# Second block: masked columns left out, and each head's values and their rests side by side in one stationary operand

## The chip, the cores and the metric

The kernel runs on one core of a Trainium2 chip. The metric is the device time of one execution in microseconds (us). The engines are TensorE (PE in the rows, its weight loads PEld), VectorE (DVE), ScalarE (ACT), GpSimd (POOL) and SyncE (SP, which issues the DMA transfers).

## The reference

Two blocks follow each other, each of two layers; 256 tokens of width 1024. The change touches the second block alone. A layer of it is a feed-forward part, a mix of three attention branches, and a second feed-forward part, each with a layer norm. The mix:

```python
o_a = _nsa(q_a, kv_a, g_a, ...)          # 8 heads in 2 groups: compressed, selected and window attention, gated
o_b = _swa_sink(q_b, k_b, v_b, sinks, rel_b)   # 8 heads in 2 groups: the last 128 keys, with a sink
o_c = _fox(q_c, k_c, v_c, f_c, b_f)            # 8 heads: causal, with a forget gate added to the logits
g = jax.nn.sigmoid(h @ w_gate + b_gate).reshape(B, S, N_BRANCH, D)
merged = g[:, :, 0] * (o_a @ w_br_a) + g[:, :, 1] * (o_b @ w_br_b) + g[:, :, 2] * (o_c @ w_br_c)
return merged @ w_out
```

All three branches are causal: a query of the first 128 tokens sees no key of the second 128. With 256 tokens the selection of branch a takes every block, so each branch is a softmax over at most 256 keys (and 30 compressed ones in a), with heads of 64 columns.

## The kernel before

Everything that TensorE multiplies in the stages of the change is held as a pair of fp32r numbers: a value rounded to fp32r (`h`, hi) and its rest (`l`, lo). `split` makes such a pair from a source with a cast on ScalarE (line 536) and a subtraction on VectorE (line 537). A product is three matmuls, hi by hi, hi by lo and lo by hi (`mm3`, lines 547 to 549). Weights come from memory in chunks of 128x1024; class `Weights` loads them and splits them too, on ScalarE (line 354) and VectorE (line 356), into five buffers in these stages.

`mix` makes the attention stages of a layer. Each of the three branches has 8 units, one for each head, in pairs j of two heads i; the two heads of a pair stand in the two halves of the 128 partitions. A unit goes through these steps, in `simple` for b and c and written out at the end of `mix` for a:

- `soft`: the scores of 2 x 128 queries against 256 keys (b: lines 1685 and 1686, in c also 1689; a: lines 1847 and 1851), then masked minimum (line 625), exponential (615, in a 1863), sum and reciprocal (616), and scaling (621, in a 1872) on VectorE and ScalarE. For the first 128 queries only the first 128 keys matter; the score matmuls make all 256 columns, and softmax reads 128 of them.
- the turn: three transposes of 128x128 (1710, in a 1883) bring the three weight tiles that are not masked into a bank; `split` brings them to `p_h` and `p_l`, into columns 128 to 511 of a buffer of `pts` whose first 128 columns were cleared once (line 1652) and stand for the masked tile.
- the values: for each of the two key tiles an `mm3` of 256 query columns, with the value columns of both heads of the pair as stationary operand (128 columns). So each unit computes the products of both heads, and half of the rows of its result are not used.
- `pair_out`, after the second head of a pair: the used half of the rows of each head is split into the branch's output pair.

Between these steps `fill` inserts matmuls of other work that doesn't depend on the unit: the projections of the next branch, the compression network, and the gated output projection of the branch before (`branch_job`). A scheduler then sets the order on each engine. The bank of the results (`po`) is a single one; the scores have two banks, the transposes two.

Of the kernel before, what the change touches and what calls it, by code (L numbers as in the profile page):

```python
# [475 lines left out]
HEAD = slice(0, 64), slice(64, 128)  # L476


class Kern:
# [979 lines left out]
    def mix(self, l, xh, xl, mid):  # L1459
        nc, fa, ra, d = self.nc, self.fa, self.ra, self.d  # L1460
        V, A, G, PE = nc.vector, nc.scalar, nc.gpsimd, nc.tensor
# [24 lines left out]
        vswb, vsh, vsl = parts(256)  # L1486
        qbb, qb = rows(512)
        kkb, kk = rows(384)
        vbb, vbh, vbl = parts(P)

        def evac0(t, ps):
            A.copy(kcv[:, t], ps[:, :256])
            self.split(ps[:, 256:], vsh[:, t], vsl[:, t])

        def evac2(t, ps):
            A.copy(kk[:, t, 0:P], ps[:, 0:P])
            self.split(ps[:, P:2 * P], vbh[:, t], vbl[:, t])
            A.copy(kk[:, t, P:], ps[:, 2 * P:])
# [9 lines left out]
        ct, pickb = ra.alloc(S), ra.alloc(8)  # L1508
        pick = pickb.a
# [3 lines left out]
        def gf_job():  # L1513
# [27 lines left out]
            for t in range(2):  # L1541
# [8 lines left out]
        vcb, vch, vcl = parts(512)  # L1550
# [3 lines left out]
                              lambda t, ps: self.split(ps, vch[:, t], vcl[:, t]))]  # L1554
# [5 lines left out]
        vcmp = ra.alloc(P)  # L1560
        self.clear(vcmp.a)
        kcmpb = ra.alloc(64)
# [23 lines left out]
        def cmp_job(z):  # L1586
            b = ftb[z]
            bank = self.banks[2]
            for c in range(4):
                hi, lo = self.W.take(f"cw{l}", 4 * z + c)  # L1590
                for jj in range(4):
                    j = 4 * c + jj
# [11 lines left out]
            ps = self.scr.next()[0:30, :S]  # L1604
# [8 lines left out]
            bank = self.pt.next()  # L1613
# [10 lines left out]
            if z == 0:  # L1624
                self.split(bank[:, 0:30], kcmpb.a[:, 0:30], kcmpb.a[:, 32:62])
            else:
                A.copy(vcmp.a[0:30], bank[0:30, 0:P])
                A.copy(vcmp.a[32:62], bank[0:30, 0:P])
                V.tensor_tensor(vcmp.a[64:94], bank[0:30, 0:P], vcmp.a[0:30].bitcast(F32), ALU.subtract)
# [43 lines left out]
        def simple(prep, vh, vl, paired, og, extra):  # L1673
# [5 lines left out]
            def soft(u):  # L1679
# [3 lines left out]
                for qt in range(2):  # L1683
                    qq, o = q[:, qt * P:qt * P + P], bank[:, qt * P:qt * P + S]
                    PE.matmul(o, qq, kh, start=True, stop=False)
                    PE.matmul(o, qq, kl, start=False, stop=extra is None)
                    if extra:
                        n = P if qt == 0 else S
                        PE.matmul(bank[:, qt * P:qt * P + n], pick[:, h:h + 1].to_broadcast([P, P]), extra[:, 0:n],
                                  start=False, stop=True)  # L1690
# [12 lines left out]
            for n, u in enumerate(units):  # L1703
# [8 lines left out]
                self.split(bank[:, 0:384], p_h.a[:, P:], p_l.a[:, P:])  # L1712
# [7 lines left out]
                c = slice(j * P, j * P + P) if paired else slice(0, P)  # L1720
                o = self.obank[:, i * S:i * S + S]
# [23 lines left out]
        simple(prep_b, vbh, vbl, False, og, None)  # L1745
# [62 lines left out]
        simple(prep_c, vch, vcl, True, og_c, ct.a)  # L1808
# [8 lines left out]
        W1 = 288  # L1817
# [23 lines left out]
        def soft(u):  # L1841
# [3 lines left out]
            for qt in range(2):  # L1845
                for z in range(2):
                    PE.matmul(bs[:, 160 * qt:160 * qt + W1], q[:, qt * P:qt * P + P], sl4[:, i, z],
                              start=z == 0, stop=z == 1)
            for qt in range(2):
                for z in range(2):  # L1850
                    PE.matmul(bw[:, P * qt:P * qt + S], q[:, qt * P:qt * P + P], wi4[:, i, z],
                              start=z == 0, stop=z == 1)
# [23 lines left out]
        for n, u in enumerate(units):  # L1876
# [3 lines left out]
            for k, (s, o, w) in enumerate(((s1, 160, 32), (s2, P, 0))):  # L1880
# [4 lines left out]
                self.split(bank[:, 0:384], pts[k][0].a[:, P:], pts[k][1].a[:, P:])  # L1885
# [77 lines left out]
```

## Time and profile before

| | before |
|---|---|
| time, median of 3 runs | 2344.83 us (2343.74 to 2349.3) |
| profiled execution, its time | 2346.41 us |
| its span, first to last instruction | 2344.6 us |
| TensorE busy | 2261.1 us, 96% |
| VectorE busy | 1696.6 us, 72% |
| ScalarE busy | 1249.1 us, 53% |
| DMA | 362.98 MB, 155 GB/s on average |
| granted TensorE clock | 0.993 |

Busy time counts a matmul from its start to its modelled end, and successive matmuls overlap, so what a matmul costs in a stream is read from the starts, not from its duration. The attention stages of the second block lie at about 1212 to 1430 us (layer 0) and 1890 to 2100 us (layer 1).

### The profile page before, as it was taken

What the parts mean: (1) busy time and instruction counts of PE and PEld (TensorE: products, weight loads), DVE (VectorE), ACT (ScalarE), POOL (GpSimd) and SP (SyncE); (2) the same over time, 40 slices, a digit from 0 to 9 for tenths busy, and PEclk for the clock granted to TensorE, in tenths of its full rate; (3) what the DMA queues carried; (4) which work ended last, traced back from release to release, by engine and by line L of the source; (5) the groups of instructions that cost most, each with busy time, mean ns of one, the idle gap of its engine ahead of it and who ended that gap; (6) DMA issues with size and microseconds to landing.
All of it is one profiled execution on the core that took longest, in us unless ns stands there. A gap on an engine that the chain in (4) does not pass through costs nothing.

```text
span 2344.6 us, 32027 instructions
## 1 busy us (share of the span) xinstructions
PE 2261.1 (96%) x11612; PEld 1858.8 (79%) x11612; DVE 1696.6 (72%) x3192; ACT 1249.1 (53%) x2235; POOL 244.0 (10%) x265
## 2 busy tenths in 40 slices
PE   6999899999999999999999999999999999999998
PEld 3888787787778899888877777788788877777887
DVE  6598999677689997655577897755655677897554
ACT  6385673242347864444367785444444376764452
POOL 1302200222220202200000000000000000000000
PEclk9999999999999999999999999999999999999999
DMA  8121224355443335555646435556556545445554
GB/s 321 45 82 41 75 81 135 126 165 168 134 139 110 103 132 171 179 186 180 220 137 205 138 117 173 179 188 197 189 190 219 163 153 184 144 131 179 189 190 134
DMA packets 102975, 362.98 MB, mean 155 GB/s; under 512 B 11936, under 2 KB 13088, under 8 KB 102304
## 3 DMA queue, kind: packets, MB, share of 16 engines
q1 hardware_dynamic: 102816, 360.93, 46.5%
q8 instruction: 91, 1.49, 0.3%
q14 instruction: 68, 0.56, 0.1%
HBM read 359.84 MB, written 1.05 MB: 154 GB/s over the span
## 4 chain that ended last, share of the span: by engine, by line
PE 55%; DVE 8%; ACT 4%; DMA 3%; issue 2%; POOL 1%; DVEq 0%; ACTq 0%; POOLq 0%; SPq 0%
PE bank L547 17%; PE bank L549 17%; PE bank L548 16%; DVE ra_t L356 2%; ACT ra_t L354 1%; DMA fa_t<-in_gate 1%; PE bank L1402 1%; DVE ra_t L537 1%; DVE fa_t L625 1%; DVE fa_t L1339 1%; DMA fa_t<-in_n 1%; PE bank L1265 1%; ACT ra_t L536 1%; POOL fa_t L543 0%; ACT fa_t L1863 0%
## 5 line engine op out<-in xcount | busy, mean ns | idle before, releaser
L547 PE MATMUL bank<-ra_t 128*128 128x512 f32 (+1 forms) x3216 | 1186.9, 371 | 14.3 <-DVE fa_t L786 5.0
L549 PE MATMUL bank<-ra_t 128*128 128x512 f32 (+1 forms) x3216 | 1172.8, 366 | 8.3 <-DVE ra_t L537 3.8
L548 PE MATMUL bank<-ra_t 128*128 128x512 f32 (+1 forms) x3216 | 1174.6, 367 | 3.8 <-DVE ra_t L537 1.3
L356 DVE TENSOR_TENSOR ra_t<-fa_t,ra_t 128x1024 fp32r<-128x1024 f32 x583 | 722.2, 1241 | 349.1 <-ACT ra_t L354 333.6
L354 ACT CAST ra_t<-fa_t 128x1024 fp32r<-128x1024 f32 x606 | 633.2, 1048 | 602.2 <-PE bank L549 284.5
L547 PEld LDWEIGHTS bank<-ra_t 128*128 128x128 f32 x3216 | 605.4, 189 | 129.1 <-ACT ra_t L536 15.4
L549 PEld LDWEIGHTS bank<-ra_t 128*128 128x128 f32 x3216 | 605.6, 189 | 108.7 <-DVE ra_t L537 7.3
L548 PEld LDWEIGHTS bank<-ra_t 128*128 128x128 f32 x3216 | 607.2, 189 | 103.1 <-DVE ra_t L356 5.1
L865 DVE SCALAR_TENSOR_TENSOR fa_t<-fa_t 128x512 f32<-128x512 f32 (+1 forms) x240 | 161.5, 673 | 6.0 <-ACT fa_t L863 2.8
L537 DVE TENSOR_TENSOR ra_t<-bank,ra_t 128x512 fp32r<-128x512 f32 (+5 forms) x234 | 131.2, 568 | 44.0 <-ACT ra_t L536 41.1
L536 ACT CAST ra_t<-bank 128x512 fp32r<-128x512 f32 (+5 forms) x234 | 112.8, 488 | 84.8 <-PE bank L549 33.4
L543 POOL TENSOR_TENSOR fa_t<-fa_t 128x1 f32<-128x1 f32 (+2 forms) x54 | 69.0, 1278 | 762.3 <-DVE fa_t L542 762.1
L625 DVE CUSTOM_DVE_ANT_0 fa_t<-bank,fa_t 128x256 f32<-128x256 f32 (+2 forms) x320 | 117.0, 396 | 8.7 <-PE bank L1231 1.9
L615 ACT ACTIVATE fa_t<-fa_t 128x257 f32<-128x257 f32 (+5 forms) x160 | 91.5, 574 | 21.4 <-DVE fa_t L625 20.1
L1410 ACT ACTIVATE fa_t<-bank 128x256 f32<-128x256 f32 x88 | 33.9, 385 | 112.5 <-PE bank L549 112.4
L356 POOL TENSOR_TENSOR ra_t<-fa_t,ra_t 128x1024 fp32r<-128x1024 f32 x23 | 58.0, 2520 | 276.1 <-ACT ra_t L354 273.0
L1412 DVE TENSOR_TENSOR fa_t<-fa_t,bank 128x256 f32<-128x256 f32 x88 | 36.8, 418 | 65.7 <-ACT fa_t L1410 65.5
L1184 DVE SCALAR_TENSOR_TENSOR fa_t<-fa_t 128x512 f32<-128x512 f32 x98 | 71.0, 757 | 2.3 <-DMA fa_t<-in_ada 2.0
L1053 POOL TENSOR_TENSOR fa_t<-fa_t 128x512 f32<-128x512 f32 (+1 forms) x32 | 37.3, 1172 | 154.4 <-DVE fa_t L1052 154.4
L638 DVE TENSOR_TENSOR ra_t<-bank,ra_t 64x256 fp32r<-64x256 f32 (+1 forms) x96 | 43.5, 455 | 8.3 <-ACT ra_t L637 5.3
L649 POOL CAST ra_t<-fa_t 64x256 fp32r<-64x256 f32 (+3 forms) x40 | 24.0, 606 | 241.4 <-PE bank L1597 69.9
L1863 ACT ACTIVATE fa_t<-fa_t 128x32 f32<-128x32 f32 (+2 forms) x96 | 39.0, 409 | 14.5 <-DVE fa_t L625 13.9
(218 smaller groups left out, 1701.9 us busy)
## 6 DMA issues: line engine op xcount, KB each, us to landing
fa_t<-in_f1w SPq DMA_DIRECT2D x132, 512.0 KB, 4.2
fa_t<-in_f2w SPq DMA_DIRECT2D x132, 512.0 KB, 4.3
fa_t<-in_tr SPq DMA_DIRECT2D x88, 512.0 KB, 3.5
fa_t<-in_n SPq DMA_DIRECT2D x56, 512.0 KB, 3.6
fa_t<-in_ada SPq DMA_DIRECT2D x48, 512.0 KB, 4.5
fa_t<-in_gate SPq DMA_DIRECT2D x48, 512.0 KB, 3.7
fa_t<-in_nat SPq DMA_DIRECT2D x36, 512.0 KB, 4.2
fa_t<-in_proj SPq DMA_DIRECT2D x24, 512.0 KB, 3.5
```

Of the source, the lines that this page charges most:

```text
L354: nc.scalar.copy(hi, raw)
L356: eng.tensor_tensor(lo, raw, hi.bitcast(F32), ALU.subtract)
L536: self.nc.scalar.copy(hi, src)
L537: self.nc.vector.tensor_tensor(lo, src, hi.bitcast(F32), ALU.subtract)
L543: self.nc.gpsimd.tensor_tensor(out, out, self.nhalf[:, :n], ALU.pow)
L547: mm(ps, lh, rh, start=start, stop=False)
L548: mm(ps, lh, rl, start=False, stop=False)
L549: mm(ps, ll, rh, start=False, stop=stop)
L615: nc.scalar.activation(s[:, :width or n], s[:, :width or n], AF.Exp, bias=mneg, scale=-1.0, accum_out=r)
L625: self.nc.vector.tensor_tensor_reduce(out=out, in0=a, in1=b, op0=ALU.add, op1=ALU.min, scale=-1.0, scalar=init, accum_out=acc)
L865: V.scalar_tensor_tensor(y4, src, w, y4, ALU.mult, ALU.add)
L1184: V.scalar_tensor_tensor(acc[s].a, wk, self.sc[:, kt, s:s + 1], acc[s].a, ALU.mult, ALU.add)
```

## The change

Three things change in `mix`, in both layers. First, the values of a head (64 columns) and their rests (64 columns) are stored side by side, as one stationary operand of 128 columns; `pairs` and `values` lay them out so that head 0 of a pair has its values in the first half and head 1 in the second. A key tile then takes two matmuls, with `p_h` and with `p_l` as moving operand, and the result has the part from the values in the head's own half of the partitions and the part from the rests in the other half; `pair_out` adds the two. (The product of rest and rest, which was left out before, is now in it.) Secondly, masked tiles are left out: scores of the first 128 queries are made for 128 keys only, and the second key tile is multiplied for the second 128 queries only, so that the cleared columns of `pts` go. Thirdly, the values of the compressed keys (`vcmp`) are laid out in the same way.

```diff
-        def parts(n):
-            b = ra.alloc(4 * n)
-            v = b.v("p (z t c) -> p z t c", z=2, t=2)
-            return b, v[:, 0], v[:, 1]
+        def pairs(n):
+            b = ra.alloc(512 * n)
+            return b, b.v("p (t j z c) -> p t j z c", t=2, j=n, z=4)
+
+        def values(src, v):
+            self.split(src.rearrange("p (j i c) -> p j i c", i=2, c=64), v[:, :, 0:4:3], v[:, :, 1:3])
...
-        pts = []
-        for i in range(2):
-            b = (ra.alloc(512), ra.alloc(512))
-            for z in b:
-                V.tensor_copy(z.a[:, 0:P], self.zero[:, 0:P])
-            pts.append(b)
+        pts = [(ra.alloc(3 * P), ra.alloc(3 * P)) for _ in range(2)]
...
+        def weigh(o, v, i, ps, start, stop):
+            st = v[:, 2 * i:2 * i + 2].rearrange("p z c -> p (z c)")
+            for k in range(2):
+                PE.matmul(o, st, ps[k], start=start and k == 0, stop=stop and k == 1)
...
-            for k, r in enumerate((slice(0, 64), slice(64, 128))):
-                self.split(bank[r, k * S:k * S + S], h[r, c], lo[r, c])
+            z = self.scr.next()[:, :S]
+            for k, (own, other) in enumerate((HEAD, HEAD[::-1])):
+                A.copy(z[own], bank[other, k * S:k * S + S])
+            for k, own in enumerate(HEAD):
+                V.tensor_tensor(z[own], bank[own, k * S:k * S + S], z[own], ALU.add)
+            self.split(z, h[:, c], lo[:, c])
...
-                    PE.matmul(o, qq, kh, start=True, stop=False)
-                    PE.matmul(o, qq, kl, start=False, stop=extra is None)
+                    n = P if qt == 0 else S
+                    PE.matmul(o, qq, kh[:, :n], start=True, stop=False)
+                    PE.matmul(o, qq, kl[:, :n], start=False, stop=extra is None)
...
-                for kt in range(2):
-                    r = slice(S - kt * S, 2 * S - kt * S)
-                    self.mm3(o, vh[:, kt, c], vl[:, kt, c], p_h.a[:, r], p_l.a[:, r], kt == 0, kt == 1)
+                for kt, r in enumerate((slice(P, 3 * P), slice(0, P))):
+                    weigh(self.obank[:, i * S + kt * P:i * S + S], v[:, kt, j if paired else 0], i,
+                          (p_h.a[:, r], p_l.a[:, r]), kt == 0, kt == 1)
...
-                    PE.matmul(bs[:, 160 * qt:160 * qt + W1], q[:, qt * P:qt * P + P], sl4[:, i, z],
+                    PE.matmul(bs[:, 160 * qt:160 * qt + 32 + n], q[:, qt * P:qt * P + P], sl4[:, i, z, :32 + n],
...
-                    PE.matmul(bw[:, P * qt:P * qt + S], q[:, qt * P:qt * P + P], wi4[:, i, z],
+                    PE.matmul(bw[:, P * qt:P * qt + n], q[:, qt * P:qt * P + P], wi4[:, i, z, :n],
...
-                for kt in range(2):
-                    r = slice(S - kt * S, 2 * S - kt * S)
-                    c = slice(k * P, k * P + P)
-                    self.mm3(o, vsh[:, kt, c], vsl[:, kt, c], pts[k][0].a[:, r], pts[k][1].a[:, r],
-                             k == 0 and kt == 0, False)
-            PE.matmul(o, vcmp.a, pc, start=False, stop=True)
+                for kt, r in enumerate((slice(P, 3 * P), slice(0, P))):
+                    weigh(o[:, kt * P:], vsw[:, kt, k], i, [z.a[:, r] for z in pts[k]], k == 0 and kt == 0, False)
+            PE.matmul(o, vcmp.a[:, i * P:i * P + P], pc, start=False, stop=True)
```

How this stands in the order of instructions is shown at two places. The first is TensorE in branch c of layer 0, around the seventh unit. In the kernel before, its six score matmuls (lines 1685, 1686 and 1689 into bank_66) are followed by these rows; bank_64 takes filler, bank_70 the values of the unit before.

```order
L1689 MATMUL bank_66<-ra_t 128x256
L547 MATMUL bank_70<-ra_t 128x256
L549 MATMUL bank_64<-ra_t 128x512
L547 MATMUL bank_64<-ra_t 128x512
L548 MATMUL bank_64<-ra_t 128x512
L549 MATMUL bank_64<-ra_t 128x512
L548 MATMUL bank_70<-ra_t 128x256
L549 MATMUL bank_70<-ra_t 128x256
L547 MATMUL bank_70<-ra_t 128x256
L548 MATMUL bank_70<-ra_t 128x256
L549 MATMUL bank_70<-ra_t 128x256
L547 MATMUL bank_64<-ra_t 128x512
```

Behind them stand the six score matmuls of the eighth unit (into bank_67) and then these rows, which end with the seventh unit's transposes.

```order
L1689 MATMUL bank_67<-ra_t 128x256
L548 MATMUL bank_64<-ra_t 128x512
L549 MATMUL bank_64<-ra_t 128x512
L547 MATMUL bank_64<-ra_t 128x512
L548 MATMUL bank_64<-ra_t 128x512
L549 MATMUL bank_64<-ra_t 128x512
L1710 MATMUL bank_68<-fa_t 128x128 x3
```

In the changed kernel these are the rows from the seventh unit's last score matmul (line 1703, before 1689) to its transposes (line 1723, before 1710), but for the first eight of them, which are four value matmuls (line 1675, of 256, 256, 128 and 128 columns) and the first four of the eighth unit's scores.

```order
L1701 MATMUL bank_67<-ra_t 128x256
L1703 MATMUL bank_67<-ra_t 128x256
L549 MATMUL bank_63<-ra_t 128x512
L547 MATMUL bank_64<-ra_t 128x512
L1723 MATMUL bank_68<-fa_t 128x128 x3
```

Six value matmuls have become four, and of ten filler matmuls of 512 columns between the scores and the transposes two are left; the others now stand elsewhere.

The second place is VectorE at `pair_out`, in the same branch. bank_70 holds the result of a pair. In the kernel before, each head's subtraction (line 537) reads the bank by itself:

```order
L537 TENSOR_TENSOR ra_t<-bank_70,ra_t 64x256
```

There are two such rows for a pair. In the changed kernel there are two additions (line 1684) and a subtraction over all partitions:

```order
L1684 TENSOR_TENSOR fa_t<-bank_70,fa_t 64x256 x2
...
L537 TENSOR_TENSOR ra_t<-fa_t,ra_t 128x256
```

The reads of the bank stay two, of the same shape, and a third instruction is added that doesn't read it.

## Rows read from the trace of the kernel before

**Rows 1.** The page: span, and busy us of each engine with its share and instructions.

```profile
span 2344.6 us, 32027 instructions
PE 2261.1 (96%) x11612; PEld 1858.8 (79%) x11612; DVE 1696.6 (72%) x3192; ACT 1249.1 (53%) x2235; POOL 244.0 (10%) x265
```

**Rows 2.** Windows: start:end, length, busy us of each engine, clock, DMA share, GB/s.

```profile
1221.00:1257.00 36.00, 34.77 (x204) 27.49 (x203) 31.18 (x101) 30.88 (x74) 3.37 (x13) 1.00 0.40 129
1257.00:1290.00 33.00, 31.15 (x161) 24.10 (x161) 22.80 (x34) 19.92 (x34) 2.53 (x4) 1.00 0.72 238
1290.00:1333.00 43.00, 41.92 (x236) 32.88 (x235) 39.28 (x117) 32.83 (x81) 1.86 (x5) 1.00 0.40 128
1350.00:1424.00 74.00, 71.28 (x407) 57.84 (x406) 67.82 (x238) 55.58 (x177) 6.15 (x4) 1.00 0.35 116
```

**Rows 3.** Chain of waits by line: 1221:1257, 1290:1333, 1350:1424.

```profile
by line: PE bank L547 14.0%; PE bank L549 13.2%; PE bank L548 12.5%; DVE ra_t L356 6.5%; PE bank L1710 5.3%; PE bank L1685 5.2%; DVE ra_t L537 5.1%; DVE ra_t L638 4.7%; DVE fa_t L625 4.3%; issue 3.8%; ACT L615 3.6%; ACT ra_t L536 3.3%; PE b
...
by line: PE bank L547 22.0%; PE bank L549 18.5%; PE bank L548 17.4%; DMA fa_t<-in_gate 8.1%; PE bank L1710 5.4%; PE bank L1685 4.6%; ACT fa_t L615 4.5%; ACT ra_t L536 3.1%; PE bank L1686 2.7%; ACT ra_t L354 2.4%; PE bank L1689 2.1%; PE bank
...
by line: PE bank L547 10.3%; PE bank L549 9.8%; PE bank L548 9.7%; DVE ra_t L356 9.1%; ACT fa_t L1863 6.9%; DVE fa_t L1872 6.3%; PE bank L1883 5.3%; issue 5.2%; ACT ra_t L536 4.0%; ACT ra_t L354 3.8%; DVE ra_t L537 3.3%; PE bank L1851 3.1%;
```

**Rows 4.** Timeline of TensorE, one unit's scores in c (start, duration, line, shapes).

```profile
1311.64 0.28 PE L1685 MATMUL bank<-ra_t 128*128 128x256 f32 x1
1311.76 0.28 PE L1686 MATMUL bank<-ra_t 128*128 128x256 f32 x1
1311.88 0.22 PE L1689 MATMUL bank<-ra_t 128*128 128x128 f32 x1
1311.94 0.33 PE L1685 MATMUL bank<-ra_t 128*128 128x256 f32 x1
1312.11 0.28 PE L1686 MATMUL bank<-ra_t 128*128 128x256 f32 x1
1312.22 0.28 PE L1689 MATMUL bank<-ra_t 128*128 128x256 f32 x1
```

**Rows 5.** Timeline of the weight loads in the same stretch.

```profile
1311.76 0.19 PEld L1689 LDWEIGHTS bank<-ra_t 128*128 128x128 f32 x1
1311.88 0.19 PEld L1685 LDWEIGHTS bank<-ra_t 128*128 128x128 f32 x1
1311.99 0.19 PEld L1686 LDWEIGHTS bank<-ra_t 128*128 128x128 f32 x1
1312.11 0.19 PEld L1689 LDWEIGHTS bank<-ra_t 128*128 128x128 f32 x1
```

**Rows 6.** Groups by line and form, VectorE and ScalarE: busy us, mean ns.

```profile
L537 DVE TENSOR_TENSOR ra_t<-bank,ra_t 64x256 fp32r<-64x256 f32 x48 | 20.2, 421 | 3.9 <-ACT ra_t L536 2.4
L537 DVE TENSOR_TENSOR ra_t<-fa_t,ra_t 128x256 fp32r<-128x256 f32 x12 | 7.0, 587 | 0.4
L1652 DVE CAST ra_t<-fa_t 128x128 fp32r<-128x128 f32 x8 | 1.8, 220 | 0.0
L356 DVE TENSOR_TENSOR ra_t<-fa_t,ra_t 128x256 fp32r<-128x256 f32 x2 | 0.8, 417 | 0.0
...
L1292 ACT COPY fa_t<-bank 64x256 f32<-64x256 f32 x48 | 17.6, 367 | 13.7 <-PE bank L549 12.8
L536 ACT CAST ra_t<-bank 64x256 fp32r<-64x256 f32 x48 | 17.6, 366 | 6.1 <-PE bank L549 4.4 <-DVE ra_t L537 1.0
L536 ACT CAST ra_t<-fa_t 128x256 fp32r<-128x256 f32 x12 | 4.9, 406 | 4.0 <-DVE fa_t L934 4.0
```

**Rows 7.** Timeline, seventh unit of c: last score, transposes, VectorE's scaling.

```profile
1321.04 0.28 PE L1689 MATMUL bank<-ra_t 128*128 128x256 f32 x1
...
1325.41 0.55 PE L1710 MATMUL bank<-fa_t 128*128 128x128 f32 x3
...
1324.63 0.73 DVE L621 TENSOR_SCALAR fa_t<-fa_t 128x128 f32<-128x128 f32 x2
```

**Rows 8.** Waits, 1290 to 1332 us: us in total, times, longest.

```profile
PEld bank L1710 <- DVE fa_t L621: 2.4, 5, 1.0
```

More of the change, by code (lines that the diff above doesn't have):

```diff
@@ L1477, in rows @@
             return b, b.v("p (t c) -> p t c", t=2)
-        def parts(n):
-            b = ra.alloc(4 * n)
-            v = b.v("p (z t c) -> p z t c", z=2, t=2)
-            return b, v[:, 0], v[:, 1]
+        def pairs(n):
[3 more added lines that the diff above has]
+            self.split(src.rearrange("p (j i c) -> p j i c", i=2, c=64), v[:, :, 0:4:3], v[:, :, 1:3])
         kcvb, kcv = rows(256)
-        vswb, vsh, vsl = parts(256)
+        vswb, vsw = pairs(2)
         qbb, qb = rows(512)
         kkb, kk = rows(384)
-        vbb, vbh, vbl = parts(P)
+        vbb, vb = pairs(1)
         def evac0(t, ps):
             A.copy(kcv[:, t], ps[:, :256])
-            self.split(ps[:, 256:], vsh[:, t], vsl[:, t])
+            values(ps[:, 256:], vsw[:, t])
         def evac2(t, ps):
             A.copy(kk[:, t, 0:P], ps[:, 0:P])
-            self.split(ps[:, P:2 * P], vbh[:, t], vbl[:, t])
+            values(ps[:, P:2 * P], vb[:, t])
             A.copy(kk[:, t, P:], ps[:, 2 * P:])
@@ L1549, in mix @@
         kcb, kc = rows(512)
-        vcb, vch, vcl = parts(512)
+        vcb, vc = pairs(4)
         fills = [self.natural(f"n2{l}", 12, 2, xh, xl, [0, 1], lambda t, ps: A.mul(qc[:, t], ps, 0.125)),
@@ L1553, in mix @@
                  self.natural(f"n2{l}", 20, 2, xh, xl, [0, 1],
-                              lambda t, ps: self.split(ps, vch[:, t], vcl[:, t]))]
+                              lambda t, ps: values(ps, vc[:, t]))]
         ch1 = fa.alloc(64)
         ftb = {}
-        vcmp = ra.alloc(P)
+        vcmp = ra.alloc(2 * P)
         self.clear(vcmp.a)
+        vcmp3 = vcmp.v("p (z c) -> p z c", z=4)[:, 0:4:3]
         kcmpb = ra.alloc(64)
@@ L1626, in cmp_job @@
             else:
-                A.copy(vcmp.a[0:30], bank[0:30, 0:P])
-                A.copy(vcmp.a[32:62], bank[0:30, 0:P])
-                V.tensor_tensor(vcmp.a[64:94], bank[0:30, 0:P], vcmp.a[0:30].bitcast(F32), ALU.subtract)
+                b3 = bank[0:30, 0:P].rearrange("p (i c) -> p i c", i=2)
+                A.copy(vcmp3[0:30], b3)
+                A.copy(vcmp3[32:62], b3)
+                V.tensor_tensor(vcmp3[64:94], b3, vcmp3[0:30].bitcast(F32), ALU.subtract)
             yield 880
@@ L1683, in soft @@
                 for qt in range(2):
-                    qq, o = q[:, qt * P:qt * P + P], bank[:, qt * P:qt * P + S]
-                    PE.matmul(o, qq, kh, start=True, stop=False)
-                    PE.matmul(o, qq, kl, start=False, stop=extra is None)
+                    n = P if qt == 0 else S
+                    qq, o = q[:, qt * P:qt * P + P], bank[:, qt * P:qt * P + n]
+                    PE.matmul(o, qq, kh[:, :n], start=True, stop=False)
+                    PE.matmul(o, qq, kl[:, :n], start=False, stop=extra is None)
                     if extra:
-                        n = P if qt == 0 else S
-                        PE.matmul(bank[:, qt * P:qt * P + n], pick[:, h:h + 1].to_broadcast([P, P]), extra[:, 0:n],
-                                  start=False, stop=True)
+                        PE.matmul(o, pick[:, h:h + 1].to_broadcast([P, P]), extra[:, 0:n], start=False, stop=True)
                 sb, ss = sr.next(), self.sm.next()
@@ L1711, in simple @@
                 p_h, p_l = pts[n % 2]
-                self.split(bank[:, 0:384], p_h.a[:, P:], p_l.a[:, P:])
+                self.split(bank[:, 0:384], p_h.a, p_l.a)
                 if i == 0 and j < 3:
@@ L1744, in mix @@
         ogb, og = new_og()
-        simple(prep_b, vbh, vbl, False, og, None)
+        simple(prep_b, vb, False, og, None)
         self.flush()
@@ L1807, in mix @@
         ogc, og_c = new_og()
-        simple(prep_c, vch, vcl, True, og_c, ct.a)
+        simple(prep_c, vc, True, og_c, ct.a)
         self.flush()
@@ L1845, in soft @@
             for qt in range(2):
+                n = P if qt == 0 else S
                 for z in range(2):
[L1847 removed]
+                    PE.matmul(bs[:, 160 * qt:160 * qt + 32 + n], q[:, qt * P:qt * P + P], sl4[:, i, z, :32 + n],
                               start=z == 0, stop=z == 1)
             for qt in range(2):
+                n = P if qt == 0 else S
                 for z in range(2):
[L1851 removed]
+                    PE.matmul(bw[:, P * qt:P * qt + n], q[:, qt * P:qt * P + P], wi4[:, i, z, :n],
                               start=z == 0, stop=z == 1)
@@ L1884, in mix @@
                 PE.transpose(bank[0:32, 384:512], s1[:, 160 * k:160 * k + 32], ident)
-                self.split(bank[:, 0:384], pts[k][0].a[:, P:], pts[k][1].a[:, P:])
+                self.split(bank[:, 0:384], pts[k][0].a, pts[k][1].a)
                 cq, bq = slice(k * P, k * P + P), bank[0:32, 384:512]
```

4 lines of the change are left out of this document (1 added, 3 removed).

## The prediction

> **What bounds the kernel now.** I read the page first, then the change's own stretches by windows, then the chain of waits in them, then single instructions. The page shows TensorE busy in 2261.1 of 2344.6 us [rows 1]: this is a kernel in which TensorE hardly rests. But the change touches only the attention stages of the second block, twice 200 us, and there the picture is closer. In layer 0 the unit phases of the three branches lie at 1221 to 1257 us (b), 1290 to 1333 us (c) and 1350 to 1424 us (a). TensorE is busy in 34.77 of 36, 41.92 of 43 and 71.28 of 74 us of them, and VectorE in 31.18, 39.28 and 67.82 us, so VectorE stands at 87%, 91% and 92%; the granted clock is 1.00 throughout [rows 2]. Two engines are nearly full at once. The chain of waits says which one sets the time: of the lines that its row names, TensorE's add up to 50% in b (14.0 + 13.2 + 12.5 + 5.3 + 5.2), 73% in c (22.0 + 18.5 + 17.4 + 5.4 + 4.6 + 2.7 + 2.1) and 38% in a (10.3 + 9.8 + 9.7 + 5.3 + 3.1) [rows 3]. VectorE's named lines hold 21%, nothing and 19%, ScalarE's 7%, 10% and 15%. Between b and c (1257 to 1290 us) the DMA engines are busy at 0.72 and move 238 GB/s [rows 2]; those transfers start when buffers come free, so time won in b moves them forward, and I count it as kept.
>
> **Fewer matmuls.** For one 128-key tile the old code issues three matmuls (value by weight, value by weight's rest, value's rest by weight), the new one two, since a head's 64 value columns and their 64 rests fill one stationary operand. A unit of b or c goes from 6 to 4, a unit of a from 12 to 8 (besides the compressed one). With 8 units per branch that is 16 + 16 + 32 = 64 fewer in a layer, 128 in both. The price of one is read from start to start in a stream: the 256-wide matmuls of a score unit begin at 1311.64, 1311.76 and 1311.88, and the sixth at 1312.22, which is 0.58 us for five [rows 4]; the weight loads say 0.117 us (1311.76 to 1312.11 for three) [rows 5], and I use that. 128 x 0.117 = 15.0 us of TensorE time go: 1.87 us in b, 1.87 in c and 3.74 in a, in each layer.
>
> **Narrow matmuls.** The new code also halves the width of the masked tiles: per layer 32 score matmuls in b and c together, 32 in a (16 of them 288 to 160) and 64 value matmuls, 256 in both layers. Kernel before already has such a matmul, the 128-wide one of line 1689 in branch c. It takes 0.22 us instead of 0.28 and the next one begins 0.06 us after it, but the one after that only 0.17 us later (1311.88, 1311.94, 1312.11) [rows 4]. The two gaps make 0.23 us, what two wide ones take. The reason stands in the weight loads: they begin at 1311.76, 1311.88, 1311.99 and 1312.11, one per 0.117 us, whatever the width of the matmul [rows 5]. So a narrow matmul with a 128-column stationary operand of its own gives back in the next gap what it saved, and I book nothing. The bound on the other side is 0.117 - 0.060 = 0.057 us for each, 14.6 us.
>
> The Trainium skill has both sides of this on one page (TensorE: Matmul & The Clock Gate): "Back-to-back issue gap" gives an isolated gap of N / 2.4 + 2.5 ns, by which 128 columns take half of 256 and these edits would be worth about 13.6 us more (an estimate from that formula), while "LDWEIGHTS (loading the stationary operand)" makes a load depend on its columns alone, some 107 ns for 128. The trace of line 1689 agrees with the second.
>
> **What comes on top.** The two halves of the result, values and rests, now stand in different partition halves and are added in pair_out: before two casts and two subtractions of 64x256, now two copies, two additions of 64x256, one cast and one subtraction of 128x256. The copy costs ScalarE what the cast did (367 and 366 ns), the addition VectorE what the subtraction did (421 ns, the same shape with one operand in a bank). New are the cast, 406 ns, and the subtraction, 587 ns by the row of its own line and operands, or 417 ns by line 356 [rows 6]; I take 500. There are 24 calls: 12.0 us of VectorE (10.0 to 14.1) and 9.7 us of ScalarE. Eight clears of 220 ns (line 1652) go, 1.8 us of VectorE. The rest is booked at nothing: the split of the values into a pattern of 64-column pieces keeps its element count (no row shows that write pattern; if such a cast or subtraction took twice its time, some 24 instructions would cost up to 0.7 us each, all of them in the filler or ahead of the units, where the engines have gaps), the clear of vcmp lies on GpSimd, and the longer way to the finished rows is hidden, since the branch's projection first runs the gate matmuls. The bank of the outputs is read until the second addition, as before until the second subtraction; the next head pair writes it a unit later.
>
> **What of it lies on the path.** I weight each engine's change by its share of the chain. TensorE: 1.87 x 0.50 + 1.87 x 0.73 + 3.74 x 0.38 = 3.7 us in a layer, 7.5 in both. VectorE has 4 x 0.5 = 2.0 us more in each branch, ScalarE 4 x 0.41 = 1.6: b 2.0 x 0.21 + 1.6 x 0.07, c 1.6 x 0.10, a 2.0 x 0.19 + 1.6 x 0.15, together 1.3 us, less 0.2 for the four clears at b's share: 1.1 in a layer, 2.3 in both.
>
> **The order.** The instructions are also put in another order, and one place in c looks worse. Softmax of the seventh unit needs about 4 us: its last score matmul begins at 1321.04, VectorE's scaling ends at 1325.36 (1324.63 + 0.73), and the transposes come at 1325.41, just in time [rows 7]. Before, TensorE had 12 matmuls of 0.117 us and 10 of 0.233 between scores and transposes, 3.7 us. Now it has 10 and 2, 1.6 us. Two other units of c go from 4.0 to 2.1 and from 3.3 to 2.6, counted in the same way. A shortfall of 2 us there is not lost whole, because VectorE and ScalarE use the wait to run ahead with the weights; waits of the transposes for softmax are 2.4 us in this stage now [rows 8]. Against the three losses (0.7 + 1.9 + 2.1 us) stands one unit with 0.6 us more, so 4.1 us in a layer at most. I book 1 us a layer, 2.0 in both, with 0 and 8.2 as ends.
>
> **The sum.** -7.5 + 2.3 + 2.0 = -3.2 us. The profiled execution took 2346.41 us (its span 2344.6 and 1.8 around it), 1.6 above the median of the runs, 2344.83. Against that median: 2341.6 us. A change under 0.3% (7.0 us) can hardly be told from none here, and this lies inside it.
>
> **The rivals.** *All of TensorE's time is kept.* For it speaks that TensorE is 97% busy even in these stages, and that the filler behind them could take up any gap. Then 15.0 us come off, the 2.3 us are hidden, and the time is 2330 us; against it, the chain names TensorE for 38% in a, where half of the saving lies. Chance 0.21, between 2330 and 2337.
>
> *Narrow matmuls pay as well.* The 14.6 us at the same shares are another 7.3 us: 2334 us, and 2315 if nothing is given back. Rows 4 and 5 speak against it, though the place they show has only one narrow matmul between wide ones, and the new code has two in a row. Chance 0.06. The skill's formula for the gap is this rival.
>
> *VectorE becomes the bound, and the kernel gets slower.* The place is the unit phase of a, where VectorE is at 92% and weight preparation (line 356, 9.1% of the chain) queues on the same engine ahead of softmax [rows 2, 3]. If the 8% of idle time can't be pressed further, nothing of TensorE's saving counts, and each branch takes its own 2.0 us: 6 us in a layer less 0.9, 10.2 in both, 2355 us. It decides as soon as the idle share stays at its present size in all three branches; in a alone it gives +4 us and stays unseen. Chance 0.14.
>
> **How the numbers follow.** The forecast, little changed at 2341.6 us, has 0.59, with 2336 to 2347 for its own range; 0.06 of it lies under the 0.3% line and 0.01 over the other one. Faster is then 0.06 + 0.21 + 0.06 = 0.33, slower 0.01 + 0.14 = 0.15, and 0.52 is left for no visible change. The range of 2330 to 2351 takes in the first rival and leaves out most of the second and the upper part of the third, about 0.2 in all.
>
> **What would show it.** Right: 128 fewer matmuls; 128-wide ones of some 0.22 us whose follower starts late, with weight loads still every 0.117 us; the unit phases of b, c and a shorter by less than 1, 1 and 2 us; VectorE's share in a above 92%, and longer waits of the transposes for softmax in c. Wrong: phases shorter by 2, 2 and 4 us with no new waits (the first rival), narrow matmuls at 0.06 us from start to start over several in a row (the second), or a phase a that is longer than 74 us with VectorE above 95% (the third).

## The result, and the profile after

The changed kernel takes 2359.19 us (median of 4 runs, 2356.63 to 2362.31), the kernel before 2345.32 us beside it (4 runs, 2343.74 to 2349.3). The ratio is 1.0057, 95% interval 1.0038 to 1.0076: some 13 to 14 us slower. The prediction was 2341.6 us in a range of 2330 to 2351, with 0.15 for slower. It was wrong.

In the changed kernel some lines have moved: scores of b and c are lines 1700, 1701 and 1703 (before 1685, 1686 and 1689), their turn 1723 (1710), the turn of a 1896 (1883), VectorE's scaling in a 1885 (1872), the value matmuls 1675, the additions in `pair_out` 1684. Its page, with span, busy times and the engines' shares of the chain that ended last; the last line is that chain for the kernel before:

```profile
span 2355.8 us, 31859 instructions
...
PE 2252.4 (96%) x11484; PEld 1841.5 (78%) x11484; DVE 1701.8 (72%) x3208; ACT 1256.2 (53%) x2259; POOL 243.7 (10%) x265
...
PE 49%; DVE 12%; ACT 6%; DMA 3%; issue 3%; POOL 1%; DVEq 0%; ACTq 0%; POOLq 0%; SPq 0%
...
PE 55%; DVE 8%; ACT 4%; DMA 3%; issue 2%; POOL 1%; DVEq 0%; ACTq 0%; POOLq 0%; SPq 0%
```

TensorE has 128 matmuls and 8.7 us of busy time less than in [rows 1], and the span is 11.2 us longer: TensorE's idle time grew from 83.5 to 103.4 us. The windows of layer 0 show where. These are the changed kernel's unit phase of b, unit phase of c, the stretch between the last turn of c and the first scores of a, the unit phase of a, the stretch from there to the merge of the branches (its first transposes, line 1928, before 1918), and the whole block, from its first transposes to the last of the merge; columns as in [rows 2].

```profile
1222.30:1260.80 38.50, 34.87 (x190) 25.96 (x191) 33.18 (x105) 31.49 (x75) 3.21 (x13) 1.00 0.38 122
1293.20:1327.60 34.40, 32.27 (x179) 24.05 (x179) 33.04 (x112) 28.52 (x77) 1.85 (x5) 1.00 0.27 91
1327.60:1353.50 25.90, 25.52 (x118) 20.46 (x117) 17.28 (x22) 15.69 (x26) 0.00 (x0) 1.00 0.58 194
1353.50:1419.90 66.40, 58.82 (x328) 45.76 (x328) 61.57 (x231) 52.44 (x170) 5.12 (x4) 1.00 0.35 112
1419.90:1436.90 17.00, 16.45 (x78) 12.93 (x77) 12.23 (x18) 9.66 (x17) 0.00 (x0) 1.00 0.51 159
1213.20:1458.80 245.60, 228.26 (x1193) 176.47 (x1192) 203.49 (x545) 177.49 (x438) 12.83 (x26) 1.00 0.46 152
```

The same six for the kernel before, cut at the same instructions:

```profile
1221.70:1259.30 37.60, 36.45 (x211) 29.14 (x212) 32.51 (x102) 30.94 (x73) 3.37 (x13) 1.00 0.41 135
1291.70:1329.50 37.80, 36.72 (x210) 29.01 (x211) 34.97 (x112) 29.85 (x76) 1.86 (x5) 1.00 0.38 126
1329.50:1350.80 21.30, 20.88 (x99) 16.63 (x98) 12.92 (x17) 11.98 (x22) 0.00 (x0) 1.00 0.53 173
1350.80:1418.70 67.90, 65.18 (x375) 53.15 (x374) 63.86 (x230) 51.25 (x167) 6.15 (x4) 1.00 0.36 119
1418.70:1431.35 12.65, 12.60 (x63) 9.93 (x62) 9.57 (x15) 8.71 (x15) 0.00 (x0) 1.00 0.57 185
1212.50:1453.30 240.80, 232.19 (x1257) 185.09 (x1256) 199.57 (x533) 173.14 (x426) 13.91 (x26) 1.00 0.47 155
```

The whole block went from 240.8 to 245.6 us (layer 1, by the starts of the same instructions: 240.7 to 245.8). In it TensorE's busy time fell by 3.9 us and its idle time rose from 8.6 to 17.3 us. The units of c and a are shorter (34.4 for 37.8 us and 66.4 for 67.9), those of b longer (38.5 for 37.6), but TensorE is idle for more of them: 7.6 us in a, before 2.7; 3.6 in b, before 1.2; 2.1 in c, before 1.1. And the stretches behind c and a, in which almost nothing runs but other work's matmuls of 512 columns, grew from 21.3 to 25.9 and from 12.65 to 17.0 us. Counted from the timeline, 154 matmuls of 512 columns stand between the first scores and the last turn of a before, 133 now; in c 88 and 70, in b 77 and 73. What is missing there stands behind the last turn: 44 became 63 behind a, 83 became 104 behind c. The total from b's first scores to the merge hardly moved (538 and 535). So the same filler runs, but later, after the units that it had covered.

The chain in the unit phases of c and a answers to the second and third line of [rows 3].

```profile
by line: PE bank L1723 8.5%; issue 7.3%; DVE fa_t L621 7.1%; DVE ra_t L638 6.8%; ACT ra_t L354 6.3%; PE bank L1675 6.0%; DVE ra_t L537 5.6%; ACT fa_t L615 5.5%; PE bank L549 4.7%; ACT ra_t L637 4.3%; PE bank L548 4.2%; PE bank L1700 3.6%; A
...
by line: DVE fa_t L1885 10.6%; ACT fa_t L1876 10.4%; DVE ra_t L356 8.8%; DVE ra_t L537 6.6%; PE bank L549 6.3%; DVE fa_t L625 5.8%; PE bank L1896 5.5%; PE bank L547 5.5%; PE bank L548 5.5%; issue 5.4%; ACT ra_t L536 4.5%; DVE ra_t L638 4.5%
```

Of the named lines in c, TensorE's hold 27% (8.5 + 6.0 + 4.7 + 4.2 + 3.6), where they held 73%, and VectorE's 20%, where they held nothing. In a the first two are now softmax itself: scaling on VectorE and the exponential on ScalarE. The waits of TensorE over the whole run say the same (us in total, times, longest):

```profile
PE bank L1896 <- DVE fa_t L1885: 7.5, 10, 1.1
...
PE bank L1914 <- ACT ra_t L1902: 4.2, 10, 0.9
...
PE bank L1723 <- DVE fa_t L621: 1.3, 4, 0.4
```

And the two waits of the turns in the kernel before:

```profile
PE bank L1883 <- DVE fa_t L1872: 4.4, 6, 0.9
...
PE bank L1710 <- DVE fa_t L621: 1.4, 4, 0.6
```

The turn of a waits 7.5 us for VectorE's scaling, before 4.4 us; the turns of b and c, 1.3 us together, no longer than before (1.4). The 4.2 us of line 1914, the product with the compressed keys' values, which waits for ScalarE's copies of line 1902, are not among the waits of the kernel before. One such place on TensorE's timeline, in brackets the idle time before the instruction and what ended it:

```profile
1417.84 0.39 PE L549 MATMUL bank<-ra_t 128*128 128x512 f32 x1
1419.38 0.55 PE L1896 MATMUL bank<-fa_t 128*128 128x128 f32 x3 [1.15 <-DVE fa_t L1885]
```

The filler matmul ahead of the turn starts at 1417.84; after it TensorE stands 1.15 us, since the turn is next in its order, although 63 filler matmuls are still to come behind it.

### The profile page after: what moved, and what is told of

Same layout as the page of the kernel before. It is cut to its first block, busy times and chain, and to the rows that moved or that the text cites. A ratio compares the mean times of both kernels' runs of the same rounds, so it can differ in the third digit from the quotient of the medians.

```text
span 2355.8 us, 31859 instructions
## 1 busy us (share of the span) xinstructions
PE 2252.4 (96%) x11484; PEld 1841.5 (78%) x11484; DVE 1701.8 (72%) x3208; ACT 1256.2 (53%) x2259; POOL 243.7 (10%) x265
## 4 chain that ended last, share of the span: by engine, by line
PE 49%; DVE 12%; ACT 6%; DMA 3%; issue 3%; POOL 1%; DVEq 0%; ACTq 0%; POOLq 0%; SPq 0%
PE bank L549 15%; PE bank L547 15%; PE bank L548 15%; DVE ra_t L356 3%; ACT ra_t L354 2%; DVE ra_t L537 1%; DVE fa_t L625 1%; DVE ra_t L638 1%; PE bank L1402 1%; DVE fa_t L865 1%; DMA fa_t<-in_gate 1%; DVE fa_t L1885 1%; ACT fa_t L1876 1%; DVE fa_t L1339 1%; PE bank L1265 1%
## 5 line engine op out<-in xcount | busy, mean ns | idle before, releaser
L547 PE MATMUL bank<-ra_t 128*128 128x512 f32 (+1 forms) x3088 | 1148.4, 373 | 13.3 <-DVE fa_t L786 5.0
L549 PE MATMUL bank<-ra_t 128*128 128x512 f32 (+1 forms) x3088 | 1139.9, 370 | 8.4 <-DVE ra_t L537 3.8
L548 PE MATMUL bank<-ra_t 128*128 128x512 f32 (+1 forms) x3088 | 1140.1, 370 | 7.1 <-DVE ra_t L356 4.5
L547 PEld LDWEIGHTS bank<-ra_t 128*128 128x128 f32 x3088 | 582.1, 189 | 113.3 <-issue 7.6
L549 PEld LDWEIGHTS bank<-ra_t 128*128 128x128 f32 x3088 | 582.5, 189 | 108.1 <-DVE ra_t L537 7.2
L548 PEld LDWEIGHTS bank<-ra_t 128*128 128x128 f32 x3088 | 583.3, 189 | 104.7 <-DVE ra_t L356 10.1
L537 DVE TENSOR_TENSOR ra_t<-bank,ra_t 128x512 fp32r<-128x512 f32 (+4 forms) x186 | 110.6, 604 | 36.5 <-ACT ra_t L536 34.9
L536 ACT CAST ra_t<-bank 128x512 fp32r<-128x512 f32 (+4 forms) x186 | 95.2, 519 | 68.2 <-PE bank L549 26.3
L1675 PEld LDWEIGHTS bank<-ra_t 128*128 128x128 f32 x256 | 37.5, 188 | 22.4 <-ACT ra_t L536 12.4
L1675 PE MATMUL bank<-ra_t 128*128 128x256 f32 (+1 forms) x256 | 50.5, 297 | 3.4 <-ACT ra_t L536 1.7
```

What stands on the lines that cost most here:

```text
L536: self.nc.scalar.copy(hi, src)
L537: self.nc.vector.tensor_tensor(lo, src, hi.bitcast(F32), ALU.subtract)
L547: mm(ps, lh, rh, start=start, stop=False)
L548: mm(ps, lh, rl, start=False, stop=False)
L549: mm(ps, ll, rh, start=False, stop=stop)
L1675: PE.matmul(o, st, ps[k], start=start and k == 0, stop=stop and k == 1)
```

## Experiments

Three theories. **Theory 1, the order:** the narrower widths and fewer matmuls make the scheduler put the instructions in another order, with less filler between the units, and that order costs the time. **Theory 2, the merge of a pair:** `pair_out`'s longer way on VectorE and ScalarE is the price (the prediction's third rival is near it). **Theory 3, the narrow matmuls:** they themselves cost more than their place shows. All times are medians; ratios are to the kernel before, run beside.

**Narrow scores alone.** The kernel before with only the score matmuls narrowed. The instructions are the same in kind and number.

```diff
-                    qq, o = q[:, qt * P:qt * P + P], bank[:, qt * P:qt * P + S]
-                    PE.matmul(o, qq, kh, start=True, stop=False)
+                    n = P if qt == 0 else S
+                    qq, o = q[:, qt * P:qt * P + P], bank[:, qt * P:qt * P + n]
+                    PE.matmul(o, qq, kh[:, :n], start=True, stop=False)
...
```

The same is done to the other score matmuls of b, c and a.

> The kernel before with one thing changed: scores of the first 128 queries are made for 128 keys only. Instructions of VectorE and ScalarE are the same, and so are TensorE's in number. Theory 1 (the order: a narrow matmul is planned as a short one, so less filler is put between the units, while on the chip it takes as long as a wide one): slower by 6 to 15 us, with fewer 512-wide matmuls in the unit phases (c 88 to about 67, a 154 to about 123) and TensorE waiting longer there. Theory 2 (the added instructions of pair_out load VectorE and ScalarE): no change, within 3 us. Theory 3 (a narrow matmul is dearer on the chip than a wide one): slower by under 3 us, with starts more than 0.12 us apart.

2356.34 us, ratio 1.0039 (1.0024 to 1.0054): one part of the change, without its new merge and with not a matmul less or more, already gives 9.2 us of its loss. Its windows behind c, units of a, and whole block:

```profile
1327.40:1354.10 26.70, 26.31 (x123) 21.42 (x121) 17.23 (x21) 15.74 (x26) 0.00 (x0) 1.00 0.59 187
1354.10:1416.80 62.70, 58.12 (x346) 47.28 (x346) 57.87 (x226) 49.10 (x165) 3.49 (x2) 1.00 0.34 106
1212.60:1459.30 246.70, 233.28 (x1257) 184.83 (x1255) 199.24 (x533) 173.22 (x426) 12.78 (x26) 1.00 0.47 151
```

The pattern is the changed kernel's: 26.7 us behind c, TensorE idle for 4.6 of 62.7 us in a, the block 246.7 us (before: 21.3, 2.7 of 67.9, and 240.8). By count, a's units hold 125 matmuls of 512 columns (154 before) and c's 69 (88).

**The pairs with all widths full.** The change, but no masked column left out: scores and values at full width, values and rests side by side, new merge.

```diff
-                for kt, r in enumerate((slice(P, 3 * P), slice(0, P))):
-                    weigh(self.obank[:, i * S + kt * P:i * S + S], v[:, kt, j if paired else 0], i,
+                for kt, r in enumerate((slice(S, 2 * S), slice(0, S))):
+                    weigh(self.obank[:, i * S:i * S + S], v[:, kt, j if paired else 0], i,
...
```

> The changed kernel with the full width kept everywhere (scores of 256 keys, the cleared columns of the weight tiles multiplied as before); values and rests side by side, two matmuls for a key tile, and the new pair_out stay. Theory 1 (order): faster than before by 7 to 15 us, 2330 to 2338, since 128 matmuls of 0.117 us are gone and the filler stays in the unit phases. Theory 2 (pair_out): slower than before by 5 to 14 us, as the changed kernel. Theory 3: faster than before, but by under 7 us.

2334.69 us, ratio 0.9945 (0.993 to 0.996): 12.4 us faster than the kernel before, and the fastest version here. The same three windows:

```profile
1328.70:1347.90 19.20, 18.67 (x88) 14.92 (x86) 13.69 (x20) 11.81 (x21) 0.00 (x0) 1.00 0.61 200
1347.90:1420.50 72.60, 69.54 (x380) 55.67 (x380) 66.25 (x237) 56.48 (x175) 6.07 (x4) 1.00 0.40 125
1212.50:1447.70 235.20, 225.95 (x1194) 177.00 (x1192) 201.43 (x545) 175.74 (x438) 13.75 (x26) 1.00 0.50 158
```

Now 185 matmuls of 512 columns lie among the units of a and only 40 behind them; the block takes 235.2 us, with TensorE idle for 9.3 us of it. Theory 2 expected this kernel to be 5 to 14 us slower, since the new merge is in it, and misses here.

**The new merge alone.** The kernel before with the change's `pair_out`: two copies, two additions, a cast and a subtraction. Its output adds the halves of the old layout and so holds other numbers.

```diff
-            for k, r in enumerate((slice(0, 64), slice(64, 128))):
-                self.split(bank[r, k * S:k * S + S], h[r, c], lo[r, c])
+            z = self.scr.next()[:, :S]
+            for k, (own, other) in enumerate((HEAD, HEAD[::-1])):
+                A.copy(z[own], bank[other, k * S:k * S + S])
+            for k, own in enumerate(HEAD):
+                V.tensor_tensor(z[own], bank[own, k * S:k * S + S], z[own], ALU.add)
+            self.split(z, h[:, c], lo[:, c])
```

> The kernel before with pair_out of the changed kernel alone: for each pair two copies, two additions, a cast and a subtraction in place of two casts and two subtractions. The halves that it adds then belong to the other head, so the branch outputs are other numbers. Theory 1 (order): slower by 0 to 4 us. Theory 2 (the added work of VectorE and ScalarE is the loss): slower by 10 to 14 us.

2345.58 us against 2347.12, ratio 0.9995 (0.9986 to 1.0005). Theory 2 expected 10 to 14 us more and misses. The price of the merge alone is not shown by this run: the scheduler set another order here too, with 159 matmuls of 512 columns in a where the kernel before has 154, and what the one costs the other may give back.

**Wide scores, narrow values.** The change with its score matmuls at full width again (the first experiment's edit, the other way).

> The changed kernel with scores of 256 keys for all queries again; the values keep the narrow tile. Theory 1 (order): the filler is back in the unit phases (c about 92, a about 159 matmuls of 512 columns), and the time is 2331 to 2341 us. Theory 2 (pair_out): as the changed kernel, 2353 to 2362 us. Theory 3 (narrow matmuls dear): about half of the changed kernel's loss is left, 2348 to 2355 us.

2340.55 us, ratio 0.9971 (0.996 to 0.9982): 18.6 us below the changed kernel, by making 128 matmuls wider. As theory 1 expected, the filler is back: 92 matmuls of 512 columns in c and 159 in a. Against the second experiment it has only the value matmuls narrow, and is 5.9 us slower, with 159 for 185 in a.

**Filler held to its unit.** To take the choice from the scheduler, filler was held behind the turn of the unit in which the code issues it, by a dependence that sets the order only. Four forms: the kernel before, narrow scores, the change, and the wide pairs.

```diff
-        while ns > 0 and self.queue:
-            try:
-                ns -= next(self.queue[0])
...
+        with self.tc.issue_after(self.turned[-1 - 0]) if len(self.turned) > 0 else nullcontext():
+            while ns > 0 and self.queue:
+                try:
+                    ns -= next(self.queue[0])
...
```

> The kernel before with the filler's place on TensorE fixed: each matmul of the filler is ordered behind the transposes of the unit in which the program issues it (an order edge on the engine, no wait). With it the count of 512-wide matmuls in the unit phases is 69 in b, 105 in c and 126 in a, in all kernels of this call. It is the base for the next three; by itself slower or faster than the kernel before by up to 15 us.

> The kernel with narrow scores alone, with the filler's place fixed in the same way. Theory 1 (the loss of 9 us comes from the changed order): within 3 us of the held kernel before. Theory 3 (the narrow matmuls themselves): slower than the held kernel before by 9 us again.

> The changed kernel with the filler's place fixed in the same way. Theory 1: faster than the held kernel before by 8 to 16 us (128 matmuls of 0.117 us fewer, little given back). Theory 2 (pair_out): slower than the held kernel before, or within 3 us.

> Values and rests side by side, all widths full, with the filler's place fixed in the same way. Theory 1: as the held changed kernel within 4 us, since a narrow matmul saves nothing in a stream. A theory in which narrow matmuls pay when the order is the same: slower than the held changed kernel by 5 to 14 us.

2415.66, 2423.52, 2421.7 and 2419.7 us; ratios 1.0298, 1.0331, 1.0321 and 1.0321, each within 0.002. All four are 70 to 78 us slower. Theory 1 misses twice here: narrow scores lie 7.9 us over the held kernel before, where it expected under 3 and theory 3 expected 9; and the held change lies 6.0 us over it, where theory 1 expected 8 to 16 us less and theory 2 allowed for this. Only the held wide pairs came as theory 1 expected, within 4 us of the held change (2.0 us below). The number of filler matmuls in the units is the same in all four (69, 105 and 126), but other instructions still stand in other places, this order brings waits of its own (14.4 us in two waits of line 1617 for VectorE, in the held kernel before), and it slows TensorE's clock. In the held kernel before, in steps of 10 us:

```profile
1270.00:1280.00 10.00, 9.43 (x50) 7.16 (x50) 6.48 (x9) 6.02 (x10) 0.39 (x1) 1.00 0.77 239
1280.00:1290.00 10.00, 6.19 (x36) 5.01 (x34) 6.68 (x8) 6.45 (x9) 0.39 (x1) 1.00 0.77 222
1290.00:1300.00 10.00, 4.55 (x19) 3.16 (x19) 5.17 (x11) 4.50 (x12) 0.00 (x0) 0.53 0.49 156
1300.00:1310.00 10.00, 8.82 (x36) 7.27 (x35) 4.99 (x21) 4.66 (x15) 0.00 (x0) 0.62 0.00 0
1310.00:1320.00 10.00, 9.82 (x60) 8.37 (x59) 7.09 (x20) 6.63 (x17) 0.00 (x0) 1.00 0.13 40
```

At 1280 TensorE falls to 6.19 busy of 10 us, and in the next steps the granted clock is 0.53 and 0.62, mostly the lower of its two levels, 1.2 of 2.4 GHz; it is 1.00 again from 1310, after 8.82 of 10 us. Over the whole run the granted clock is 0.977 in the held kernel before and 0.973, 0.973 and 0.975 in the other three, 0.993 in the kernel before. As a share of the span that is 55, 65, 65 and 60 us not granted, 16 in the kernel before (an estimate from these clocks and spans, such as 0.023 x 2411.6; an upper bound on what the clock costs, since TensorE also idles). The clock can thus hold over half of the 70 us and all the differences within the set, so the set does not decide between the theories. What it does show is that another order, with the clock that comes with it, can be worth several times all the matmuls in question.

**The orders written out.** So the whole order was pinned: for every engine the instructions were chained by order-only dependences, in a sequence taken from another kernel.

```diff
+        for a, b in zip(seq, seq[1:]):
+            tc.add_manual_dep(at[f"I-{b}"], f"I-{a}", info, reason="pinned")
```

First the narrow scores in the order of the kernel before. In this run and the next, TensorE, VectorE and ScalarE run the same sequence from first to last as the kernel that the order is taken from.

> The kernel before with its diagonal score matmuls narrow (the first experiment's instructions), but with the order of the kernel before written out for every engine: the same instructions stand in the same places, only the widths differ. Theory 1 (the order that the scheduler makes out of narrower widths costs the time, not the widths): within 4 us of the kernel before, 2341 to 2350. Theory 3 (the narrow matmuls themselves are dearer than their place shows): as slow as the first experiment, 2353 to 2359.

2345.37 us against 2345.74, ratio 1.0001 (0.9991 to 1.0011). The loss of the first experiment is gone, and no gain shows. Windows behind c, units of a, whole block:

```profile
1329.60:1350.80 21.20, 20.78 (x98) 16.57 (x97) 12.86 (x17) 11.86 (x22) 0.00 (x0) 1.00 0.53 174
1350.80:1418.70 67.90, 64.87 (x375) 52.85 (x375) 63.82 (x230) 51.17 (x167) 6.15 (x4) 1.00 0.37 118
1211.10:1453.40 242.30, 231.77 (x1257) 184.43 (x1255) 199.82 (x533) 173.17 (x426) 13.71 (x26) 1.00 0.48 154
```

Then the reverse, the kernel before at full width in the order of the narrow scores.

> The kernel before, all score matmuls at full width, but with the order of the first experiment (narrow scores) written out for every engine. Theory 1 (the order costs the time): 2352 to 2360, as the first experiment. Theory 3 (the narrow matmuls themselves): 2343 to 2349, as the kernel before.

2355.91 us, ratio 1.0045 (1.0029 to 1.006).

```profile
1326.90:1353.60 26.70, 26.29 (x124) 21.45 (x122) 17.23 (x21) 15.76 (x26) 0.00 (x0) 1.00 0.61 187
1353.60:1416.20 62.60, 58.38 (x346) 47.58 (x346) 57.85 (x226) 49.11 (x166) 3.50 (x2) 1.00 0.35 107
1211.10:1457.90 246.80, 234.14 (x1257) 185.61 (x1256) 199.15 (x533) 172.69 (x426) 12.76 (x26) 1.00 0.48 151
```

With the first experiment the two make a square. In the old order wide and narrow take 2345.7 and 2345.4 us, in the new one 2355.9 and 2356.3. The order is worth some 9 to 11 us (the first experiment by its own kernel before, 9.2), the width of the 128 score matmuls nothing that can be measured. Theory 3 falls for them.

Third, the whole change in the order of the wide pairs.

> The whole change, narrow matmuls and all, in the order that the scheduler makes for its full-width form (the second experiment), written out for every engine. Theory 1 (the order costs the time): 2330 to 2340, the whole loss of the change gone and the second experiment's gain kept. Theory 2 (the longer merge of a pair on VectorE and ScalarE) and theory 3 (the narrow matmuls themselves): no better than 2352.

2340.38 us, ratio 0.9973 (0.9962 to 0.9984): 18.8 us below the change with the same instructions (by the ratios 0.9973 for 1.0057), and 0.4 us outside theory 1's range.

```profile
1333.20:1352.40 19.20, 18.65 (x89) 14.91 (x87) 13.66 (x20) 11.84 (x22) 0.00 (x0) 1.00 0.62 200
1352.40:1424.80 72.40, 68.81 (x379) 54.90 (x379) 66.05 (x237) 56.31 (x175) 6.06 (x4) 1.00 0.40 124
1217.00:1452.50 235.50, 224.87 (x1195) 175.85 (x1193) 201.37 (x545) 175.65 (x438) 13.81 (x26) 1.00 0.51 158
```

The block takes 235.5 us, that of the wide pairs 235.2 (layer 1: 236.3 and 235.2). So within the change's own stages the order gives back nearly all; the 256 narrow matmuls, of scores and of values, cost at most 0.3 and 1.1 us there. The 5.7 us that remain over the wide pairs are 8.7 us between the two profiled executions (spans of 2341.6 and 2332.9 us), and 7.3 of these lie outside the blocks. At 1176 to 1195 us, ahead of the first block, the two orders are not the same, and transposes of line 1315, in other parts of the layers, wait longer over the run, 6.8 us where the wide pairs have 1.1. The granted clock also falls there, to 0.83 in 1180 to 1190 us, where the wide pairs have 1.00. First the pinned change, then the wide pairs:

```profile
PE bank L1315 <- DVE fa_t L1346: 6.8, 4, 2.8
...
PE bank L1315 <- DVE fa_t L1346: 1.1, 2, 0.6
```

**The change with the old merge.** The products of the weights with the values' rests are then left out of the output; VectorE and ScalarE have the old work.

> The whole change with the old, shorter merge of a pair; the products of the weights with the values' rests are left out of the output, so that VectorE and ScalarE have the work of the kernel before in it. Scheduler's own order, which has less filler between the units than the change (67 wide matmuls in c, 120 in a). Theory 1 (order): still slow, 2352 to 2362. Theory 2 (the merge's added work is what costs): about 2346.

2355.58 us, ratio 1.004 (1.0029 to 1.0052), still slow without the merge's work. Theory 2 expected 2346 and misses again. The scheduler puts even fewer matmuls of 512 columns among the units here, 67 in c and 120 in a, and yet the time is 3.6 us under the change; the two intervals overlap, so whether the merge's work is in that is not shown.

## Why the prediction was wrong

**The step that failed is "The order".** It booked +2.0 us, with 8.2 as its upper end. The order cost the change 18.8 us against the same instructions in the order of the wide pairs. That order has more filler in the units than the kernel before (185 in a for 154), against which the term was booked; the order of the kernel before itself can't be pinned on the change, whose instructions are others. The nearest measure against it is the square, where the order that follows from narrow scores alone costs 9 to 11 us, over the upper end already. Two faults lie in the step. It looked at units of c alone, where it counted the rows between scores and turn; the counts for the three units that lose come out of the traces (the eighth, from 5.0 to 3.5 us by the same count, it leaves out), but the turns of b and c together wait no longer than before, and TensorE's idle time grew most where it didn't count: from 2.7 to 7.6 us in the units of a and from 1.2 to 3.6 in those of b. And it priced only the wait at the turn. It did not ask where filler goes that no longer stands between scores and turn: behind the branch, where it runs while VectorE and ScalarE, done with the softmax, stand idle for a third of the time and more (busy 17.28 and 15.69 of 25.9 us behind c). The upper end was a bound for c, not for the kernel.

**Fewer matmuls** held: 128 went, and in the pinned change TensorE's busy time in the block is 224.87 us for 232.19, 7.3 us less, where 64 x 0.117 = 7.5 was booked. That a share of only one half would reach the end, by **the chain's shares** (7.5 of 15.0), looks too low: the wide pairs won 12.4 us. But that run has an order of its own, with more filler in the units, so the share in a fixed order was not measured.

**Narrow matmuls at nothing** held for the matmuls themselves, now also for several in a row. In the changed kernel, three narrow score matmuls and the wide ones behind them:

```profile
1320.48 0.30 PE L1700 MATMUL bank<-ra_t 128*128 128x128 f32 x1
1320.63 0.27 PE L1701 MATMUL bank<-ra_t 128*128 128x128 f32 x1
1320.73 0.28 PE L1703 MATMUL bank<-ra_t 128*128 128x128 f32 x1
1320.85 0.33 PE L1700 MATMUL bank<-ra_t 128*128 128x256 f32 x1
1321.02 0.28 PE L1701 MATMUL bank<-ra_t 128*128 128x256 f32 x1
```

They start 0.15, 0.10 and 0.12 us apart, 0.37 us for three, as the wide ones do; durations of 0.27 to 0.30 us are no shorter, where the prediction's sign was some 0.22. The pinned square says it in time: 0.4 us between wide and narrow. The Trainium skill's "LDWEIGHTS (loading the stationary operand)" (TensorE: Matmul & The Clock Gate), by which a load depends on its columns alone, agrees with these starts. On the same page of the Trainium skill, "Back-to-back issue gap" gives 56 ns for 128 columns (N / 2.4 + 2.5) as the gap of an isolated matmul and says itself that this is too little in a stream with loads; it does not hold here, and the measurement decides. What the step missed is that a width that costs nothing on the chip was not nothing to the scheduler.

**The merge** was booked at +2.3 us and measured at no change (-3.3 to +1.2 us by the interval of its run), in an order of the scheduler's own. What it costs in a fixed order was not measured.

**The rivals.** The third one forecast 2355 us and so came near the time, but not by its mechanism: it has VectorE's work in `pair_out` as the price, yet the kernel before doesn't get slower with that work (2345.58 us), the change stays slow without it (2355.58 us), and with it the pinned change is fast (2340.38 us). Its sign didn't come either: a is 66.4 us long, not longer, and VectorE is busy for 61.57 us of that, 93%, before for 63.86 of 67.9, 94%. Half of it is true: with less filler in them, the softmax on VectorE and ScalarE leads the chain in the units of a. The first rival, all of TensorE's time kept, forecast 2330 us; the wide pairs, without the narrow widths, reached 2334.7.

**Left open:** why the scheduler spreads less filler when a matmul is narrower. Only that it does so is shown, by the first and the fourth experiment. Open is also how the change's loss divides between the narrow scores and the narrow values, since neither was pinned to the other's order alone.

## What to carry to other kernels

Where a scheduler sets the order, an edit that costs nothing in a fixed order can still move everything around it, as 128 narrower matmuls did here; compare the order of the two kernels over whole stages, count the independent work that stands among the dependent steps, and ask where the rest of it will run. If a part of a change is worth nothing by its own rows, leave it out: here the narrow widths gave nothing that could be measured, and the order that came with them cost more than the part that paid had won (2359.19 us with them, 2334.69 without). To tell an instruction's price from its order's, pin the order of one kernel on the other, in both directions.

## What the runs showed of the hardware

At a granted clock of 1.00, TensorE took a new stationary operand of 128 columns and a matmul of 128 or 256 columns about every 0.12 us (three in 0.37 us here, loads 0.117 us apart in [rows 5]); halving the columns shortened neither the starts nor the kernel (2345.4 against 2345.7 us in one order). In the held order TensorE's pauses cost clock on top: the granted clock fell to 0.53 after a step with 6.19 of 10 us busy, and was back after one with 8.82. In the changed kernel's windows it stayed at 1.00, so none of the loss in them is the clock's.
